# A hybrid retention and HGRN2 step: other pools for the last retention chunk, moved side work and loads, state updates in the output banks

## The chip, the cores and the metric

The kernel runs on one core of one Trainium2 chip. The metric is the device time of one execution in microseconds (us): the median of several runs. The engines are TensorE (PE in the profile; PEld is its weight load), VectorE (DVE), ScalarE (ACT), GpSimd (POOL) and SyncE (SP), which here issues most of the DMA transfers. PE works from on-chip memory (SBUF) into PSUM, which the kernel divides into four pools of two banks each.

## The reference

One layer mixes 2048 prompt tokens and 8 single decode tokens, with 1024 features. Eight projections of 512 columns feed two groups of four heads: retention with a fixed decay for each head, and HGRN2 with a learned decay for each token and feature. Their outputs are normalised, gated, joined and projected again.

```python
h = rmsnorm(x, norm_g)
p = (h @ w_in).astype(jnp.float32)          # 1024 x 4096
rq, rk, rv, rg, hq, hf, hi, hgate = jnp.split(p, 8, axis=-1)
rq, rk = rotary(rq, pos), rotary(rk, pos) * RET_DK ** -0.5
o_ret, s_ret_new = chunked_decay_recurrence(rq, rk, rv, log_gamma, s_ret)
o_ret = head_rmsnorm(o_ret, ret_g) * jax.nn.silu(rg)
logf = jnp.logaddexp(jnp.log(lbf), jnp.log1p(-lbf) + jax.nn.log_sigmoid(hf))
kin = (1.0 - lbf) * jax.nn.sigmoid(-hf)
o_hg, s_hg_new = chunked_decay_recurrence(silu(hq), kin, hi, logf, s_hg)
o_hg = head_rmsnorm(o_hg, hg_g) * jax.nn.silu(hgate)
y = x + jnp.concatenate([o_ret, o_hg], axis=-1) @ w_out      # then rmsnorm
# chunked_decay_recurrence: S_t = diag(f_t) S_{t-1} + k_t v_t^T ;  o_t = S_t^T q_t
```

Both the outputs and the new states of prompt and samples are returned.

## The kernel before

Every large product is made of float32 operands that are cut in two: `hi_lo` (L114) lets ACT copy the operand to a high part and DVE subtract that from the operand to get the low part, and `split` (L118) does so for a weight tile. A product is then three matmuls, high by high, high by low and low by high (`three`, L330).

The program has three stages. **Stage 1** is a loop over 24 token pairs, eight for each of three weight sets. A pair (`v_pair`) makes seven products of 12 matmuls of 512 columns each (the list `CHAIN`, named a to g in the tiles `pv18a` and so on), a scheme of the Strassen kind. The code of L864 to L930 hangs all other work of stage 1 on a list `after[n]`: what stands there is issued after product n of the pair (a half counts as in the middle). So the next weight set is loaded and summed (`wg_load`, `wg_spool`), the decode tokens get their matmuls by the raw weights (`wg_decode`, tile `pgd`, L576), the operands of the next pair are split (`s_split`), and the rotation table of the next pair is loaded into the single buffer `rot` (L361).

With the third set, 16 chunks of 128 tokens of the retention are woven in, two for each pair (`r_steps`, L775): `r_load` brings the chunk's `rq`, `rv` and `rg` into one buffer each (L704), `r_flip` transposes the keys (`pkt`), `r_score` multiplies keys and queries (`par`, L717) and masks the result on DVE (`rA`, L719), `r_update` makes the new part of the state (`pur`), `r_out` makes the output (`por`, L730 and L732) and updates the state `rS` on DVE (L736), `r_norm` normalises the output (`obr`, L752), which needs the square sums of ACT and two steps of POOL (`omr`, L744), and `r_turn` transposes it (`potr`, L760). The last chunk, 15, lies behind the last pair, among the first matmuls of stage 2.

**Stage 2** has eight units, two halves of the prompt by four heads. A unit multiplies its two weight tiles by the split activations (`pjfh` and `pjqh`, L966). Between these matmuls `merge` puts the recurrence of the unit before: the products of the levels inside of a chunk (`plh`, L1174 and L1224), fed by DVE and ACT (`kh` L1144, `qqh` L1147, `kept` L1154), and the tail (`tail_steps`): `uu` makes the state updates (`puh`, L1049) in a bank of the pool `ps_lv` that it shares with the levels, DVE chains them into states (`sth`, L1057), and `oo` makes the outputs in `ps_o`. The activations lie in four blocks; those of block 1 (`x_split`, low part `xl`) are made at the start of unit 0, before its second half needs them.

The list `side_at` (L1348) places side work at fractions of a unit: 4.8 is at 80% of unit 4. It holds the decode states of the four HGRN2 heads (`d_load`, two `d_mul`, `d_add`, `d_mm`) and the sums of the output weights for stage 3 (`t_load_raw`, four `t_sum`, `t_spool`, `t_store`). **Stage 3** projects the outputs: four plain chunks (`out_steps`, `py`, L1548), each from the outputs read back from memory (tile `or`) and split (`oc_h`, `oc_l`), and then six token pairs by seven products again.

PE follows the order of the program as written. DVE, ACT, SP and POOL are put in order by a scheduler from the waits and its model; `behind(f)` (L124) ties the instructions of f behind the last ones that DVE, ACT and SP had so far. Each engine then runs its list strictly in order, and SP's list is that of its DMA queue's issues. All loads of raw weights, states and activations share the pool `rawp` of six buffers.

Of the kernel before, what the change touches and what calls it, by code (L numbers as in the profile page):

```python
# [18 lines left out]
P = 128  # L19
# [22 lines left out]
def step_kernel(ctx, tc, a, out):  # L42
# [99 lines left out]

    def w_load():
        if len(w_ready) < len(want):
# [7 lines left out]
            r = rawp.tile([P, D], F32, tag="raw", name=f"wr{n}")  # L152
            sp.dma_start(r, a["w_in"][j])
            w_ready.append(split(r, f"w{n}_"))
# [210 lines left out]
    def v_pair(i, after):  # L365
# [8 lines left out]
        def emit(c, ty, ps, plus):  # L374
            key = n_set == 2 and ty == 0
            if key:
                pl, tag = (abp, "zh0") if c % 2 else (vq, "rk")
# [317 lines left out]
    def r_begin():  # L695
        for x, tag in (("kT", "zl0"), ("rA", "zh1"), ("rS", "zl1")):
            zz[x] = abp.tile([P, GW], F32, tag=tag, name=x)
# [29 lines left out]
    def r_out(c):  # L727
# [11 lines left out]
        o = vq.tile([P, GW], F32, tag="vo", name=f"obr{c}", bufs=3)  # L739
# [27 lines left out]
    def r_last():  # L767
        sf = vq.tile([P, GW], F32, tag="vo", name="sf", bufs=3)
# [6 lines left out]
    def r_steps(p):  # L775
# [20 lines left out]
        if p == N_V - 1:  # L796
            put(6, lambda: r_flip(ca + 1))
        if p:
            put(0.5 if p > 1 else 1.5, lambda: r_turn(ca - 2))
        if p < N_V:  # L800
# [46 lines left out]
    def d_mm(hd):  # L847
        S, vb = dec["l", hd]
        ty, h = divmod(hd, NH)
        sp.dma_start(out[("new_ret_sample", "new_hgrn_sample")[ty]][0, :, h].rearrange("b d v -> d b v"), S)  # L850
# [8 lines left out]
        for i in range(2):  # L859
            sp.dma_start(d_dram[hd, i::2], e[i : i + 103 : 34, i * P : i * P + P])  # L860
# [3 lines left out]
    for i in range(2, n_tok):  # L864
# [164 lines left out]
    def tail_steps(half, hd, acol, qcol, vcol, kT, decay, box, eps, gcol, name, ksb, ns):  # L1029
# [320 lines left out]
    for hd, at in zip(range(NH, 2 * NH), (4.8, 5.4, 6.0, 6.6)):  # L1350
# [489 lines left out]
```

## Time and profile before

| | us |
|---|---|
| runs | 1065.56, 1071.47, 1071.89 |
| median | 1071.47 |
| profiled execution | 1070.63 |
| its span in the trace | 1068.8 |
| PE busy | 1036.6 |
| DVE busy | 764.0 |
| ACT busy | 549.6 |
| POOL busy | 128.5 |

The profile shows one execution. Its span runs from the first to the last instruction; the 1.8 us to the execution's own time lie around it. Busy times are sums of intervals, and an instruction counts as busy while it runs, at whatever clock. In the views, L717 is line 717 of the kernel before, `A <- B` in a list of waits says that an instruction on A waited for one on B, and a name such as `pv18a` stands for the tile that is written. Stage 1 lies at 0 to about 590 us, stage 2 at about 580 to 915, stage 3 behind it.

### The profile page before, as it was taken

The numbers are of one execution on the slowest core, as the hardware profiler recorded it, in microseconds if no ns is written. First come the engines' busy times: TensorE is split into PE (matmuls) and PEld (weight loads), VectorE is DVE, ScalarE is ACT, GpSimd is POOL, SyncE is SP. The second block draws the span as 40 slices with busy tenths as digits, with TensorE's granted clock in tenths as the row PEclk, the third lists the DMA queues.
The fourth block names the chain that finished last, engine by engine and source line by source line (L and its number), as shares of the span: only waits on it lengthen the run. The fifth ranks groups of instructions, "written<-read, shape, count | busy, mean of one in ns | idle before, by whom it ended". The sixth has DMA issues, their size and how long they took to land.

```text
span 1068.8 us, 21293 instructions
## 1 busy us (share of the span) xinstructions
PE 1036.6 (97%) x8231; PEld 853.6 (80%) x8231; DVE 764.0 (71%) x1404; ACT 549.6 (51%) x1203; POOL 128.5 (12%) x224
## 2 busy tenths in 40 slices
PE   9999999999999999999999999999999999999997
PEld 7778678887778788788888888897777777888775
DVE  6886775987667976667657677867666687468785
ACT  7853445543344755544555565565455384433241
POOL 0310101000001011111111100011011012221122
PEclk9999999999999999999999999999999999999999
DMA  8689999568768775767677399673736465496642
GB/s 290 212 299 331 327 336 321 216 245 287 272 217 289 289 234 168 227 210 200 226 242 234 147 308 319 224 232 130 227 120 200 165 205 165 133 352 201 234 159 99
DMA packets 147270, 248.27 MB, mean 232 GB/s; under 512 B 10752, under 2 KB 78608, under 8 KB 146912
## 3 DMA queue, kind: packets, MB, share of 16 engines
q1 hardware_dynamic: 139696, 221.37, 61.9%
q0 software_dynamic: 7328, 25.27, 6.2%
q8 instruction: 65, 1.06, 0.4%
q14 instruction: 37, 0.30, 0.1%
q10 hardware_dynamic: 144, 0.26, 0.1%
HBM read 162.32 MB, written 84.54 MB: 231 GB/s over the span
## 4 chain that ended last, share of the span: by engine, by line
PE 66%; DMA 11%; DVE 9%; ACT 7%; issue 4%; POOL 1%; SPq 1%; DVEq 0%; POOLq 0%; ACTq 0%
PE po L332 11%; PE pjfh L966 5%; PE pjqh L966 4%; PE py L1548 3%; DMA rq<-qt_dram 2%; DMA xn<-in_x_prompt 2%; DMA qt_dram<-qt 2%; DMA wgr<-in_w 2%; PE par L717 1%; PE por L730 1%; PE plh L1174 1%; PE por L732 1%; PE pur L724 1%; PE puh L1049 1%; PE pv22a L332 1%
## 5 line engine op out<-in xcount | busy, mean ns | idle before, releaser
L966 PE MATMUL pjfh<-xh,w_h 128*128 128x512 f32 (+2 forms) x160 | 61.1, 382 | 0.1
L966 PE MATMUL pjqh<-xh,w_h 128*128 128x512 f32 (+2 forms) x160 | 59.8, 374 | 0.0
L1154 ACT ACTIVATE kepth<-kh 128x1024 f32<-128x1024 f32 x24 | 25.4, 1059 | 66.9 <-DVE kh L1144 62.6
L966 PE MATMUL pjfh<-xl,w_h 128*128 128x512 f32 (+2 forms) x160 | 56.9, 355 | 1.7 <-DVE xl L116 1.7
L966 PE MATMUL pjqh<-xh,w_l 128*128 128x512 f32 (+2 forms) x160 | 56.5, 353 | 1.5 <-DVE w_l L116 1.5
L966 PE MATMUL pjfh<-xh,w_l 128*128 128x512 f32 (+2 forms) x160 | 56.6, 354 | 0.0
L966 PE MATMUL pjqh<-xl,w_h 128*128 128x512 f32 (+2 forms) x160 | 56.2, 352 | 0.0
L1144 DVE TENSOR_TENSOR kh<-kh,fph 128x512 f32<-128x512 f32 x48 | 33.4, 695 | 23.8 <-PE plh L1174 14.8
L752 DVE SCALAR_TENSOR_TENSOR obr<-por,omr,rg 128x128 f32<-128x128 f32 x64 | 18.1, 345 | 34.9 <-POOL omr L744 32.5
L116 DVE TENSOR_TENSOR ab_l<-xr,ab_h 128x512 fp32r<-128x512 f32 (+1 forms) x40 | 37.5, 953 | 5.4 <-ACT ab_h L115 5.3
L115 ACT ACTIVATE ab_h<-xr 128x512 fp32r<-128x512 f32 (+1 forms) x40 | 32.3, 839 | 12.7 <-DVE xr L286 12.6
L1076 DVE SCALAR_TENSOR_TENSOR obh<-poh,orsh,v 128x128 f32<-128x128 f32 x64 | 18.0, 345 | 26.2 <-POOL orsh L112 23.7
L966 PEld LDWEIGHTS pjfh<-xh,w_h 128*128 128x128 f32 x160 | 30.7, 192 | 6.8 <-issue 2.5
L966 PEld LDWEIGHTS pjqh<-xh,w_l 128*128 128x128 f32 x160 | 30.3, 189 | 6.2 <-DVE w_l L116 1.9
L966 PEld LDWEIGHTS pjfh<-xl,w_h 128*128 128x128 f32 x160 | 30.7, 192 | 5.0 <-DVE xl L116 2.3
L966 PEld LDWEIGHTS pjfh<-xh,w_l 128*128 128x128 f32 x160 | 30.7, 192 | 4.3
L966 PEld LDWEIGHTS pjqh<-xh,w_h 128*128 128x128 f32 x160 | 30.2, 189 | 4.0 <-issue 0.4
L286 DVE SCALAR_TENSOR_TENSOR xr<-xr,g_in,rb 128x256 f32<-128x256 f32 x64 | 26.7, 479 | 8.7 <-DMA xr<-in_x_t 6.2
L1147 DVE TENSOR_TENSOR qqh<-qqh,fph 128x512 f32<-128x512 f32 x48 | 32.8, 684 | 0.0
L966 PEld LDWEIGHTS pjqh<-xl,w_h 128*128 128x128 f32 x160 | 30.3, 190 | 2.9
L762 ACT ACTIVATE obr<-potr,pk 128x128 f32<-128x128 f32 x64 | 18.5, 367 | 23.6 <-PE potr L760 23.6
L1638 DVE SCALAR_TENSOR_TENSOR xro<-xro,yms,fg 128x1024 f32<-128x1024 f32 (+1 forms) x13 | 15.6, 1203 | 20.5 <-POOL yms L112 20.5
(1835 smaller groups left out, 3406.5 us busy)
## 6 DMA issues: line engine op xcount, KB each, us to landing
xr<-a_dram SPq DMA_DIRECT2D x24, 512.0 KB
S<-s_dram SPq DMA_DIRECT2D x24, 512.0 KB
xn<-in_x_prompt SPq DMA_DIRECT2D x32, 256.0 KB
xr<-in_x_t SPq DMA_DIRECT2D x16, 512.0 KB
a_dram<-xr SPq DMA_DIRECT2D x16, 512.0 KB
s_dram<-S SPq DMA_DIRECT2D x16, 512.0 KB
wgr<-in_w SPq DMA_DIRECT2D x16, 512.0 KB
xr<-a_dram SPq DMA_DIRECT2D x32, 256.0 KB
```

Source lines behind the costliest of these rows:

```text
L115: act.activation(h, src, AF.Copy)
L116: dve.tensor_tensor(l, src, h.bitcast(F32), op=ALU.subtract)
L286: dve.scalar_tensor_tensor(r[:, k], r[:, k], g_in[:, kk : kk + 1], spread_to[i], op0=ALU.mult, op1=ALU.mult)
L332: pe.matmul(ps, xx, ww, start=(first and n == 0), stop=(last and n == 2), skip_group_check=more)
L752: dve.scalar_tensor_tensor(o[:, cc], po[:, h], ms[:, h : h + 1], rb_of[c, "g"][:, cc], op0=ALU.mult, op1=ALU.mult)
L762: act.activation(o[:, cc], pt[:, h], AF.Copy, scale=ng[:, h : h + 1])
L966: pe.matmul(ps, ww[:, kk], x[:, k, b0 : b0 + n], start=(k == 0 and i == 0), stop=(k == KT - 1 and i == 2),)
L1076: dve.scalar_tensor_tensor(ob[g][:, j], po[:, j], rs[:, j : j + 1], gcol(4 * g + j), op0=ALU.mult, op1=ALU.mult)
L1144: dve.tensor_tensor(kv[:, :, 0, :], kv[:, :, 0, :], two[:, :, 1:2].to_broadcast([P, nb, b]), op=ALU.mult)
L1147: dve.tensor_tensor(qv[:, :, 1, :], qv[:, :, 1, :], two[:, :, 0:1].to_broadcast([P, nb, b]), op=ALU.mult)
L1154: act.activation(ss[:, 512:], k[:, :HALF], AF.Copy)
L1548: pe.matmul(ps, o[:, kk], w[:, k % 4, i * 512 : (i + 1) * 512], start=(k == 0 and n == 0), stop=(k == KT - 1 and n == 2),)
```

## The change

What it does, by parts:

1. **Pools.** The tiles `kT`, `rA`, `rS` and the odd chunks' keys (tags z) move from the pool `abp` to `vq`, and the last chunk's `obr` and `sf` to `rawp`. So `abp` can be closed, and the memory of activation block 1 opened, before the last retention chunk. The splits of block 1 (`x_steps(1)`) are now issued one by one among the first steps of unit 0, and one split of block 0 moves there. `obr` of the last chunk is normalised earlier and transposed later.
2. **Weights.** The load of a weight tile (`w_fetch`) is separate from its split.
3. **Retention.** For pairs 1 to 6 of the third set the first chunk's `r_score` and `r_update` stand after product 5 instead of 4.5; for pairs 1 to 7 `r_out` and the loads of the second chunk's `rq` and `rv` stand after product 6 instead of 5.5.
4. **Decode.** `wg_decode` and `wg_spool` stand after product 4 instead of 3. The small stores of `d_mm` go to POOL's queue for the HGRN2 heads.
5. **State updates.** `puh` is taken from `ps_o` instead of `ps_lv`.
6. **Side work.** `side_at` gets other times, and the steps of one head or one quarter stand further apart.
7. **Output stage.** The loads of w_out's rows and of the first two chunks `or` stand in unit 7, ahead of the splits that use them; in stage 3 the loads and splits of later chunks are separate as well.

```diff
-    vt = vctx.enter_context(tc.tile_pool(name="vt", bufs=1))
     actx = ExitStack()
+    vt = actx.enter_context(tc.tile_pool(name="vt", bufs=1))
...
-    a21 = [[abp.tile([P, 4, P], F32R, tag=f"z{t}{n}", name=f"a21{t}{n}") for t in "hl"] for n in range(2)]
+    a21 = [[vq.tile([P, 4, P], F32R, tag=f"z{t}{n}", name=f"a21{t}{n}") for t in "hl"] for n in range(2)]
...
-        o = vq.tile([P, GW], F32, tag="vo", name=f"obr{c}", bufs=3)
+        if c < 2 * N_V - 1:
+            o = vq.tile([P, GW], F32, tag="vo", name=f"obr{c}", bufs=3)
+        else:
+            o = rawp.tile([P, GW], F32, tag="raw", name=f"obr{c}")
...
-            put(4.5 + d, lambda: r_score(ca), lambda: r_update(ca))
+            put(5 if 0 < p < N_V - 1 else 4.5 + d, lambda: r_score(ca), lambda: r_update(ca))
             if p:
-                put(5.5, lambda: r_out(ca), lambda: r_load(ca + 1, "q"), lambda: r_load(ca + 1, "v"))
+                put(6, lambda: r_out(ca), lambda: r_load(ca + 1, "q"), lambda: r_load(ca + 1, "v"))
+        if p == N_V - 1:
+            put(6, lambda: r_flip(ca + 1))
...
+        q = pool if ty else sp
...
-            sp.dma_start(d_dram[hd, i::2], e[i : i + 103 : 34, i * P : i * P + P])
+            q.dma_start(d_dram[hd, i::2], e[i : i + 103 : 34, i * P : i * P + P])
...
-                after[3] += [lambda m=m, k=j - 3: wg_decode(m, k), lambda m=m, k=j - 3: wg_spool(m, k)]
+                after[4] += [lambda m=m, k=j - 3: wg_decode(m, k), lambda m=m, k=j - 3: wg_spool(m, k)]
...
-            for kp in range(4):
-                after[2 + kp] += [lambda kp=kp: behind(lambda: x_split(0, kp, x_raw[0, kp]))]
-            after[4] += [w_load]
+            for kp, at in enumerate((1.5, 2.5, 3.5, 7)):
+                if at > 6:
+                    continue
+                after.setdefault(at, [])
+                after[at] += [lambda kp=kp: behind(lambda: x_split(0, kp, x_raw[0, kp]))]
+            after[4] += [w_fetch]
...
-            pu = ps_lv.tile([P, 4, P], F32, tag="lv", name=f"pu{name}{g}")
+            pu = ps_o.tile([P, 4, P], F32, tag="o", name=f"pu{name}{g}")
...
-    for hd, at in zip(range(NH, 2 * NH), (4.8, 5.4, 6.0, 6.6)):
+    for hd, at, mm in zip(range(NH, 2 * NH), (5.1, 5.45, 6.1, 6.45), (0.68, 0.43, 0.68, 0.43)):
-        for f, d in zip(steps, (0, 0.06, 0.085, 0.11, 0.32)):
+        for f, d in zip(steps, (0, 0.1, 0.17, 0.24, mm)):
-    for k, at in enumerate((0.4, 1.0, 1.8, 2.5)):
+    for k, at in enumerate((0.35, 1.35, 2.35, 4.35)):
-        for f, d in zip(steps, (0, 0.1, 0.115, 0.13, 0.145, 0.17, 0.25, 0.25, 0.33)):
+        for f, d in zip(steps, (0, 0.12, 0.18, 0.24, 0.3, 0.4, 0.48, 0.5, 0.58)):
...
+    side_at += [*((7.35 + 0.02 * n, f) for n, f in enumerate(wo0[1])),
+                (7.3, lambda: o_load(0)), (7.48, lambda: o_split(0)), (7.8, lambda: o_load(1)),
+                (7.7, wo1[1][0]), (7.85, wo1[1][1])]
...
-        (7, 1): lambda: wo_steps(0),
+        (7, 1): lambda: [wo0[0]] + [lambda j=j: behind(wo0[2][j]) for j in range(4)],
...
-            for n, f in enumerate(early[:8]):
-                f()
-                if n in (0, 1, 2, 4):
-                    tail_f.pop(0)()
-            r_last()
             actx.close()
...
             x_alloc(1)
-            for f in x_steps(1) + early[8:]:
+            side1 = [lambda: x_split(0, 3, x_raw[0, 3]), w_load] + x_steps(1)
+            behind(side1.pop(0))
+            for n, f in enumerate(early):
                 f()
-            r_norm(2 * N_V - 1)
-            tail_f.pop(0)()
+                if n in (0, 1, 2, 5):
+                    tail_f.pop(0)()
+                if n == 5:
+                    r_last()
+                    r_norm(2 * N_V - 1)
+                for f in side1[: 2 if n < 3 else 1]:
+                    behind(side1.pop(0))
             scan_pools()
+            fill.insert(8, (0, tail_f.pop(0)))
...
-    o_load(0)
-    o_load(1)
-    wo1 = wo_steps(1)
+    o_split(1)
     wo1[0]()
```

How the instructions move shows at three places. On SP at the end of the last token pair, around the loads for the last retention chunk (`rq`, `rv`, `rg`), the order before is this; `w_kept` are stores of split weights, `wr` a raw weight tile, `wot` raw output weights, and `kg_dram<-vo` the last pair's two output stores:

```order
L166 DMA w_keptl<-w_l 128x1024
L153 DMA wr_5598<-in_w_in 128x1024
L704 DMA rq_5428<-qt_dram 128x512
L704 DMA rv_5430<-v_dram_95 128x512
L1270 DMA wot_5675<-in_w_out 128x1024
L704 DMA rg_5483<-qg_dram_100 128x512
L1482 DMA fg<-in_final_norm_g 128x1024
L166 DMA w_kepth<-w_h 128x1024
L326 DMA kg_dram_104<-vo_5438 128x512
L326 DMA kg_dram_104<-vo_5443 128x512
```

The same place in the change, where `xr` are raw activations (its line numbers are shifted by the added lines, here by 7):

```order
L711 DMA rv_5312<-v_dram_95 128x512
L711 DMA rq_5310<-qt_dram 128x512
L711 DMA rg_5348<-qg_dram_100 128x512
L186 DMA xr_5465<-a_dram_109 128x2x256
L186 DMA xr_5465<-a_dram_110 128x2x256
L711 DMA rv_5440<-v_dram_95 128x512
L333 DMA kg_dram_104<-vo_5403 128x512
L333 DMA kg_dram_104<-vo_5408 128x512
L711 DMA rq_5438<-qt_dram 128x512
L711 DMA rg_5486<-qg_dram_100 128x512
L173 DMA w_kepth<-w_h 128x1024
```

The load of the last chunk's `rq` (5428 before, 5438 now) stood ahead of the two stores and now stands behind them; `wot` and the final norm's `fg` are gone from here.

On DVE at the start of unit 0, where block 1 is split (`xl<-xr`, `w_l` is the second weight tile's low part), the last chunk's work stands before as follows:

```order
L719 SCALAR_TENSOR_TENSOR rA<-par_5507,pk 128x128 x4
L736 SCALAR_TENSOR_TENSOR rS<-rS,pur_5516 128x128 x4
L770 TENSOR_SCALAR sf<-rS 128x128 x4
L752 SCALAR_TENSOR_TENSOR obr_5549<-por_5536,omr_5550,rg_5483 128x128
L116 TENSOR_TENSOR xl_5586<-xr_5462,xh_5585 128x2x512
L116 TENSOR_TENSOR xl_5586<-xr_5465,xh_5585 128x2x512
L116 TENSOR_TENSOR xl_5586<-xr_5468,xh_5585 128x2x512
L116 TENSOR_TENSOR xl_5586<-xr_5471,xh_5585 128x2x512
L116 TENSOR_TENSOR xl_5586<-pk,xh_5585 128x8x8
L752 SCALAR_TENSOR_TENSOR obr_5549<-por_5536,omr_5550,rg_5483 128x128 x3
```

And in the change:

```order
L957 MEMSET Ah 128x1024
L116 TENSOR_TENSOR xl_5186<-xr_5196,xh_5185 128x2x512
L116 TENSOR_TENSOR w_l<-wr_5350,w_h 128x1024
L116 TENSOR_TENSOR xl_5474<-xr_5456,xh_5473 128x2x512
L726 SCALAR_TENSOR_TENSOR rA<-par_5520,pk 128x128
L116 TENSOR_TENSOR xl_5474<-xr_5459,xh_5473 128x2x512
L116 TENSOR_TENSOR xl_5474<-xr_5462,xh_5473 128x2x512
L726 SCALAR_TENSOR_TENSOR rA<-par_5520,pk 128x128 x3
L116 TENSOR_TENSOR xl_5474<-xr_5465,xh_5473 128x2x512
L116 TENSOR_TENSOR xl_5474<-pk,xh_5473 128x8x8
L743 SCALAR_TENSOR_TENSOR rS<-rS,pur_5529 128x128 x4
L780 TENSOR_SCALAR sf<-rS 128x128 x4
```

Block 1's splits (`xl_5586` before, `xl_5474` now) stood behind all of the last chunk's state work; now they begin ahead of its `rA`, one by one between the masks, and `obr` of the last chunk comes last.

On DVE between units 6 and 7, ahead of the last unit's levels, the order before has the split of the first output chunk (`oc_l`) in the middle of the level work:

```order
L1137 COPY dech_8959<-fph_8951 128x8
L1019 TENSOR_TENSOR qqh_8571<-pjqh_512_8859,qsh_8947 128x512
L1021 TENSOR_TENSOR qqh_8571<-qqh_8571,fh_8569 128x512
L116 TENSOR_TENSOR oc_l<-or_9446,oc_h 128x1024
L1144 TENSOR_TENSOR kh_8570<-kh_8570,fh_8569 128x512
L1147 TENSOR_TENSOR qqh_8571<-qqh_8571,fh_8569 128x512
L1194 TENSOR_TENSOR Abh_8976<-pah_8977,pk 128x256
```

In the change:

```order
L1151 COPY dech_8959<-fph_8951 128x8
L1033 TENSOR_TENSOR qqh_8569<-pjqh_512_8849,qsh_8947 128x512
L1035 TENSOR_TENSOR qqh_8569<-qqh_8569,fh_8567 128x512
L1158 TENSOR_TENSOR kh_8568<-kh_8568,fh_8567 128x512
L1161 TENSOR_TENSOR qqh_8569<-qqh_8569,fh_8567 128x512
L1208 TENSOR_TENSOR Abh_8976<-pah_8977,pk 128x256
L1194 COPY_PREDICATED Abh_8976<-lmask,pah_8977 128x128
```

The split has left this place, so that `kh` follows `qqh` directly.

More of the change, by code (lines that the diff above doesn't have):

```diff
@@ L141, in step_kernel, with w_fetch @@
     w_used = [0]
+    w_raw = {}
+    def w_fetch():
+        n = len(w_ready)
+        w_raw[n] = rawp.tile([P, D], F32, tag="raw", name=f"wr{n}")
+        sp.dma_start(w_raw[n], a["w_in"][want[n]])
     def w_load():
@@ L151, in w_load @@
                 return
-            r = rawp.tile([P, D], F32, tag="raw", name=f"wr{n}")
-            sp.dma_start(r, a["w_in"][j])
-            w_ready.append(split(r, f"w{n}_"))
+            if n not in w_raw:
+                w_fetch()
+            w_ready.append(split(w_raw.pop(n), f"w{n}_"))
             for t, x in zip(w_ready[-1], w_kept):
@@ L696, in r_begin @@
         for x, tag in (("kT", "zl0"), ("rA", "zh1"), ("rS", "zl1")):
-            zz[x] = abp.tile([P, GW], F32, tag=tag, name=x)
+            zz[x] = vq.tile([P, GW], F32, tag=tag, name=x)
     heads = [slice(h * P, (h + 1) * P) for h in range(NH)]
@@ L767, in r_last @@
     def r_last():
-        sf = vq.tile([P, GW], F32, tag="vo", name="sf", bufs=3)
+        sf = rawp.tile([P, GW], F32, tag="raw", name="sf")
         for h, cc in enumerate(heads):
@@ L795, in r_steps @@
             put(5, lambda: r_turn(cb))
-        if p == N_V - 1:
-            put(6, lambda: r_flip(ca + 1))
         if p:
@@ L1403, in unit @@
                 if (i, n) in sides:
-                    group = weave(group, sides[i, n](), 0.0, 1.0 if i != 3 or n == 1 else 0.6)
+                    group = weave(group, sides[i, n](), 0.0, 1.0 if i not in (3, 7) or (i, n) == (3, 1) else 0.6)
                 steps += group
@@ L1521, in junk @@
         return pools["tp"].tile([P, 512], F32, tag="tmp", name=f"yj{junks[0]}")
-    oc = {}
-    def o_load(c):
-        r = rawp.tile([P, 8, P], F32, tag="raw", name=f"or{c}")
-        sp.dma_start(r, o_dram[:, :, c * P : (c + 1) * P].rearrange("h p t -> p h t"))
-        oc[c] = split(r.rearrange("p h t -> p (h t)"), f"oc{c}_")
     def out_steps(c):
@@ L1551, in part @@
                     )
+            if (kh, i, s) == pairs[1] + (1,) and c + 2 < PLAIN:
+                o_load(c + 2)
+            if (kh, i, s) == pairs[3] + (0,) and c + 2 < PLAIN:
+                behind(lambda: o_split(c + 2))
             if (kh, i, s) == pairs[1] + (0,):
@@ L1705, in step_kernel @@
     fill = place(fill, sorted([
-        *((0.02 + 0.04 * n, s) for n, s in enumerate(wo1[1:])),
+        *((0.02 + 0.04 * n, lambda s=s: behind(s)) for n, s in enumerate(wo1[2])),
+        (0.03, wo1[1][2]), (0.07, wo1[1][3]),
         (0.2, d_norm), (0.6, t2_load), (0.65, lambda: op_load(p0)), (0.75, lambda: op_s12(p0)),
```

29 lines of the change are left out of this document (17 added, 12 removed).

## The prediction

> **What bounds the kernel now.** I read the page first, then the list of PE's waits, then windows and timelines around the longest of them. The page's span, busy times and the foot of its chain:
>
> ```profile
> span 1068.8 us, 21293 instructions
> PE 1036.6 (97%) x8231; PEld 853.6 (80%) x8231; DVE 764.0 (71%) x1404; ACT 549.6 (51%) x1203; POOL 128.5 (12%) x224
> PE 66%; DMA 11%; DVE 9%; ACT 7%; issue 4%; POOL 1%; SPq 1%; DVEq 0%; POOLq 0%; ACTq 0%
> ```
>
> PE is busy for 97% of the span. The change leaves PE's 8231 instructions as they are in number and shape, so it can move only what PE does not work: 1068.8 − 1036.6 = 32.2 us at the most, and the time lost at a low clock, which hides inside the busy time. PE's waits, grouped by what released them (total, times, longest):
>
> ```profile
> PE puh L1049 <- DVE sth L1057: 3.8, 4, 1.4
> PE pgd L576 <- DMA wgr<-in_w: 2.7, 5, 0.6
> PE par L717 <- DMA rq<-qt_dram: 2.4, 4, 1.2
> PE plh L1174 <- ACT kepth L1155: 2.3, 1, 2.3
> PE pjfh L966 <- DVE xl L116: 1.7, 2, 1.6
> PE pjqh L966 <- DVE w_l L116: 1.5, 1, 1.5
> PE puh L1049 <- issue: 1.1, 1, 1.1
> PE pkh L1041 <- DVE kh L1144: 1.0, 1, 1.0
> PE plh L1224 <- DVE qqh L1147: 0.9, 1, 0.9
> PE py L1548 <- DVE wol L1442: 0.9, 1, 0.9
> PE por L730 <- DVE rA L719: 0.6, 1, 0.6
> PE par L717 <- DVE xl L116: 0.6, 1, 0.6
> PE plh L1174 <- DVE Abh L1180: 0.6, 1, 0.6
> ```
>
> No wait is long; the loss is some twenty small ones, each where an edit of this change lies. Two of them cost more than they show. The windows (length, busy time of PE, PEld, DVE, ACT and POOL, then the granted clock, the DMA share and GB/s) behind the waits of 1.6 and 2.3 us:
>
> ```profile
> 590.00:600.00 10.00, 8.26 (x47) 6.69 (x46) 5.48 (x13) 6.57 (x16) 1.98 (x3) 0.97 0.44 162
> 600.00:610.00 10.00, 10.00 (x74) 9.98 (x74) 6.83 (x13) 3.98 (x11) 0.81 (x1) 0.86 0.07 28
> 845.00:849.00 4.00, 4.00 (x16) 3.43 (x16) 1.36 (x6) 1.32 (x3) 0.00 (x0) 0.57 0.03 9
> ```
>
> The clock lost is 10 × 0.03 + 10 × 0.14 = 1.7 us in the first place, and 4 × 0.43 = 1.7 us in the second.
>
> A wait also costs its restart. PE's timeline around the last pair (start, duration, tile):
>
> ```profile
> 569.83 0.39 PE L332 MATMUL pv23e<-B22l,s231h 128*128 128x512 f32 x1
> 570.06 0.39 PE L332 MATMUL pv23e<-B22h,s231l 128*128 128x512 f32 x1
> 571.04 1.13 PE L717 MATMUL par<-rq,kT 128*128 128x128 f32 x8 [0.59 <-DVE xl L116]
> 578.70 0.48 PE L332 MATMUL pv23c<-T1h,s231h 128*128 128x512 f32 x1
> 580.17 0.60 PE L709 MATMUL pkt<-ident,rk 128*128 128x128 f32 x4
> 580.53 0.48 PE L966 MATMUL pjfh<-xh,w_h 128*128 128x512 f32 x1
> ```
>
> Undisturbed matmuls start 570.06 − 569.83 = 0.23 us apart; across the wait it is 0.98. The loss is 0.75 where the wait is put at 0.59, so each wait costs 0.16 us more.
>
> **The change part by part: what goes.** *State updates in ps_o.* The second `puh` of a unit waits for a bank that DVE's chain of states still reads:
>
> ```profile
> 653.19 1.23 DVE L116 TENSOR_TENSOR w_l<-wr,w_h 128x1024 fp32r<-128x1024 f32 x1
> 654.82 0.32 DVE L1057 SCALAR_TENSOR_TENSOR sth<-sth,dech,puh 128x128 f32<-128x128 f32 x1
> 655.20 1.16 PE L1049 MATMUL puh<-v,ksh 128*128 128x128 f32 x8 [1.38 <-DVE sth L1057]
> ```
>
> The chain ends at 655.14, drawn out by a split of 1.23 us in its middle, and `puh` starts right behind. In `ps_lv` the banks go pa, pu, pl, pu, so the second pu takes the first one's bank back; in `ps_o` the two updates take both banks one after the other, and what held them is the unit before's output. All five waits go, 3.8 + 1.1 = 4.9 us; and the levels, which no longer share, lose the 0.6 of `Abh`. What is late next is `poh`, which takes the first update's bank and also needs the states that come out of it, so its own operands hold it as long as the bank does.
>
> *Decode matmuls* one product later: 12 matmuls × 0.23 = 2.8 us more for a load that was at most 0.6 late. Of 2.7 us I keep 0.3.
>
> *Retention.* `par` comes 6 matmuls later (half a product, 1.4 us), against a longest wait of 1.2: the 2.4 us for `rq` go. At the last pair x's splits come half a product sooner, which takes the 0.6 of `par` on `xl` and the 0.6 of `por` on `rA`.
>
> *Block 1 split sooner.* Before, DVE makes the four low parts in one stretch, behind the last chunk:
>
> ```profile
> 596.48 4.62 DVE L116 TENSOR_TENSOR xl<-xr,xh 128x1024 fp32r<-128x1024 f32 x4
> ```
>
> Now the first of them stand ahead of that chunk's `rA`, so the waits of 1.7 on `xl` go, with the first fall of the clock. The 1.5 on `w_l` goes as its load is taken off its split.
>
> *Output loads and splits apart.* In unit 7 the split of `or` sits in ACT's and DVE's lists ahead of the levels, and its load is late:
>
> ```profile
> 831.50 7.90 DMA or<-o_dram
> 840.51 1.22 DVE L116 TENSOR_TENSOR oc_l<-or,oc_h 128x1024 fp32r<-128x1024 f32 x1 [4.18 <-ACT oc_h L115]
> 842.43 1.06 ACT L1154 ACTIVATE kepth<-kh 128x1024 f32<-128x1024 f32 x1 [1.96 <-DVE kh L1144]
> 844.10 0.74 PE L1174 MATMUL plh<-kepth 128*32 128x16 f32 x64 [2.26 <-ACT kepth L1155]
> ```
>
> DVE stood for 4.18 us, then `kh`, `kepth` and `plh` came late. In the new order the split is no longer there: the 2.3 go, with the second fall of the clock. The new split stands about half a unit behind its load, some 20 us against 7.9.
>
> *Side work spread.* Of `pkh` 1.0, `qqh` 0.9 and `py` 0.9, each behind queued side work or a late split, I take half, 1.4.
>
> The sum: 4.9 + 2.4 + 2.4 + 1.7 + 0.6 + 0.6 + 1.5 + 2.3 + 0.6 + 1.4 = 18.4 us of waits. They are about 22.5 in number, × 0.16 = 3.6 for restarts, and 3.4 for the clock: 25.4 us.
>
> **What comes.** *`potr` of chunk 14.* Its `por` moves half a product nearer to its turn. The rows above show `por` giving way at 578.70, and DVE:
>
> ```profile
> 581.59 1.13 DVE L752 SCALAR_TENSOR_TENSOR obr<-por,omr,rg 128x128 f32<-128x128 f32 x4 [2.23 <-POOL omr L744]
> ```
>
> `obr` ends at 582.72, 4.0 us after `por`. Between the two PE now has 12 matmuls, 2.8, and `pkt`, 580.53 − 580.17 = 0.4: 0.9 us of new wait; nothing below zero, since `por` cannot finish later for it.
>
> *`rq` of chunk 15* stands behind two output stores in SP's list, which wait for the last product:
>
> ```profile
> 586.59 0.92 SPq L326 DMA_DIRECT2D kg_dram<-vo  x2
> 447.73 5.63 DMA rq<-qt_dram
> ```
>
> Issued at 587.5 and landing 5.6 later, at 593.1, it can hold PE for 0 to 2 us, as `por` of this chunk stands about there now; I take 0.7.
>
> *The units.* Side work has the same instructions at other times, and its new neighbours can be hit as the old were. Bounds are 0 and 8.9, the sum of the six unit waits above whose releaser stood behind side work or late splits, with `py` (1.7 + 1.5 + 2.3 + 1.0 + 0.9 + 0.9 = 8.3) and `Abh` (0.6). I take three waits like `pkh`, 3.0 us, the small ones of the list.
>
> With 0.4 for their restarts new waits are 5.0 us. *At nothing* I put: the stores of `d_mm` on POOL, which is busy for 12%; `rq` in the other pairs, which comes behind the rotation table in SP's list (its cover is the stretch between that and `par`, priced as a rival below); and block 1's memory opened sooner, whose tiles' last readers are the last pair's matmuls, ahead on PE anyway.
>
> 25.4 − 5.0 = 20.4. The profiled execution becomes 1070.6 − 20.4 = 1050.2. It lies 0.8 under the median of the runs, so the forecast is 1051.
>
> **The rivals.** *The clock falls stay.* The waits go and the falls turn up elsewhere, after other small ones: 3.4 us more, 1054.4. For it: PE keeps small waits, and nothing shows how small is safe. Against: the falls came behind waits of 1.6 and 2.3 us, and the stretch with the wait of 1.5 on `w_l` kept its clock at 1.00:
>
> ```profile
> 626.00:636.00 10.00, 8.51 (x163) 6.50 (x162) 8.64 (x15) 5.98 (x11) 0.00 (x0) 1.00 0.81 286
> ```
>
> The Trainium skill ("TensorE: Matmul & The Clock Gate", What's actually happening) says that the clock halves after an idle window of about 3.4 us in a window that runs free. By that rule neither fall would have come from a wait of 1.6 or 2.3 us alone, and removing these need not remove the falls; the trace disagrees with it on the size of the gap, and agrees on the length of the slow stretch: 4 × 0.43 / 0.5 = 3.4 us.
>
> *Side work only changes place.* DVE keeps its 764 us and ACT its 550, so the unit waits come back at other tiles. Of the gains in units (4.9 + 1.7 + 1.5 + 2.3 + 0.6 + 1.4 = 12.4, with about 2 of restarts and 3.4 of the clock) 70%, less the 3.0 already counted, come back: some 10 us, 1062 with rounding. Against: the puh waits have a bank as their cause, not a place.
>
> *All goes and nothing comes*: 1070.6 − 25.4 + 0.8 = 1046, and 1045 with the other half of `pkh` and its like.
>
> *Slower: `rq` behind the rotation table.* Seven pairs now issue the second chunk's `rq` behind `rot` on SP, and `rot`, with its one buffer, waits for DVE's rotation of the pair before:
>
> ```profile
> 430.08 0.87 SPq L704 DMA_DIRECT2D rq<-qt_dram  x1
> 435.82 0.33 SPq L361 DMA_DIRECT2D rot<-in_rot  x1
> 441.23 1.05 PE L717 MATMUL par<-rq,kT 128*128 128x128 f32 x8
> ```
>
> If `rot` comes no sooner than now, `rq` is issued at 436.15. With 5.63 us it lands at 441.8, 0.6 after `par`; with the 7.9 of the `or` load at 444.0, 2.8 after. Beyond 2.3 us a wait brings a fall of the clock too: 2.8 + 1.7 + 0.2 = 4.7 in each pair, × 7 = 33 us, 1084. It decides from about 2.3 us of lateness on, and makes the kernel slower than before where it passes 20.4 / 7 = 2.9 us a pair. Against: `por` now comes later, so DVE turns the product before `obr`, and `rot` comes one to two us sooner; `rq` then lands about 1 us ahead of `par`.
>
> **How the numbers follow.** The forecast gets 0.57, all gone 0.08, the clock rival 0.10, side work 0.19, the slower rival 0.06. One per cent, about what a measurement can tell from no change, is 10.7 us: faster lies below 1060.8. The first three are faster, 0.75; side work is within one per cent, 0.19; the last is slower, 0.06. The range goes from 1044, a us below the case in which all goes, to 1066, four us above the side-work case for what the unit bound leaves (8.9 where 3.0 is taken); it leaves out the slower rival and some of the tails.
>
> **What would show it.** In the changed kernel: no `puh` wait on `sth`; `pgd` and `par` waits under 0.5 us in all; a clock of 0.99 in both windows; PE idle within the span down by about 17 us; a wait of about 1 at `potr` near the end of the last pair. Waits of `par` on `rq` of over 2 us in each pair would show the slower rival, and new waits at `plh`, `pkh` or `pjfh` of over 9 us together the side-work one.

## The result and the profile after

| | before | changed |
|---|---|---|
| median of 20 runs, us | 1070.84 | 1064.48 |
| lowest and highest, us | 1065.56, 1075.86 | 1060.70, 1067.43 |
| span of the profiled execution, us | 1068.8 | 1062.7 |

The ratio is 0.994, with a 95% interval of 0.9926 to 0.9954: 6.4 us faster, where 20 were forecast. The head of the page of the changed kernel:

```profile
span 1062.7 us, 21303 instructions
PE 1037.7 (98%) x8231; PEld 855.2 (80%) x8231; DVE 762.9 (72%) x1404; ACT 548.5 (52%) x1203; POOL 132.9 (13%) x232
```

PE is busy 1.1 us longer than before with the same instructions; the windows below show three stretches at a low clock where the kernel before had two (beside one at the very end in both). PE's idle time fell from 32.2 to 25.0 us, by 7.2 where about 17 were forecast. The waits of PE in the changed kernel (total, times, longest):

```profile
PE pv8a L339 <- ACT s L379: 2.1, 1, 2.1
PE pkt L716 <- DVE rk L364: 2.1, 1, 2.1
PE pv4a L339 <- ACT u L379: 1.9, 1, 1.9
PE plh L1188 <- ACT kepth L1169: 1.5, 1, 1.5
PE plh L1188 <- DVE Abh L1194: 1.5, 1, 1.5
PE pah L1206 <- DVE qqh L1035: 1.3, 1, 1.3
PE pv2b L339 <- DVE ab_l L116: 1.2, 1, 1.2
...
PE py L1572 <- DVE wol L1460: 1.0, 3, 0.4
PE pv8b L339 <- ACT wv_h L115: 0.9, 1, 0.9
PE pv8b L339 <- DVE wv_l L116: 0.8, 1, 0.8
PE plh L1238 <- DVE qqh L1161: 0.4, 1, 0.4
```

What the list of before led with is gone: no `puh`, no `pgd`, no `par` on `rq`, no `pjfh` on `xl`, no `pjqh` on `w_l`. In their place stand waits in stage 1 that the list of before does not have: `pv4a`, `pv8a`, `pv8b`, and a longer `pkt` (2.1 against 0.4). Windows of the changed kernel over the three new places and over the two old falls of the clock (the columns are those of the prediction's windows):

```profile
105.00:125.00 20.00, 18.11 (x84) 13.76 (x83) 14.48 (x25) 8.59 (x17) 2.15 (x3) 0.91 0.86 324
185.00:205.00 20.00, 16.27 (x64) 11.94 (x63) 17.13 (x21) 14.10 (x17) 0.39 (x1) 0.91 0.83 324
365.00:385.00 20.00, 17.76 (x83) 14.35 (x82) 15.96 (x22) 10.67 (x18) 0.00 (x0) 0.91 0.61 203
590.00:610.00 20.00, 19.79 (x137) 17.94 (x136) 14.12 (x28) 12.51 (x32) 2.80 (x4) 1.00 0.63 224
840.00:850.00 10.00, 10.00 (x128) 8.65 (x121) 4.92 (x12) 5.07 (x14) 0.58 (x1) 1.00 0.02 8
```

Both old falls are gone (1.00 in the last two rows), and there are three new ones, each 20 × 0.09 = 1.8 us. Where the time went shows best in the starts of the stages, read off PE's timeline: the start of the first matmul of a pair (`pv4a` for pair 4), of unit 0 (`pjfh`) and of stage 3 (`py`), and the end of the last matmul, in us. The letter in `pv4a` is that of the product's bank in PSUM, and not, as was said ahead, that of the product: products are counted from 0, and products 0, 2, 4 and 6 of pair 4 all go by `pv4a`. The last two columns belong to experiments below.

| | before | changed | e1_sums_back | e12_rotd_early |
|---|---|---|---|---|
| pair 4 | 98.16 | 98.96 | 98.66 | 99.54 |
| pair 5 | 120.41 | 123.50 | 120.23 | 124.14 |
| pair 8 | 182.83 | 184.48 | 183.61 | 184.76 |
| pair 9 | 202.93 | 210.97 | 203.70 | 204.88 |
| pair 16 | 349.85 | 356.94 | 350.32 | 351.75 |
| pair 17 | 373.21 | 383.63 | 374.84 | 375.82 |
| pair 23 | 550.29 | 557.12 | 548.12 | 550.04 |
| unit 0 | 580.53 | 585.73 | 576.73 | 579.17 |
| stage 3 | 874.89 | 867.93 | 861.43 | 861.67 |
| end | 1061.33 | 1055.18 | 1048.64 | 1048.88 |

The changed kernel loses 2.3 us in pair 4 (the differences are 0.8 ahead of it and 3.1 behind), 6.4 in pair 8 and 3.3 in pair 16. It wins 3.6 in pairs 17 to 22, 1.6 in pair 23 and 12.2 in the units, and loses 0.8 in stage 3. So most of the gains came, and 12 us that the prediction did not have went against them in stage 1.

### The profile page after: what moved, and what is told of

Its sections match the earlier page's. It is cut to its first block, busy times and chain, and to the rows that moved or that the text cites. A ratio compares the mean times of both kernels' runs of the same rounds, so it can differ in the third digit from the quotient of the medians.

```text
span 1062.7 us, 21303 instructions
## 1 busy us (share of the span) xinstructions
PE 1037.7 (98%) x8231; PEld 855.2 (80%) x8231; DVE 762.9 (72%) x1404; ACT 548.5 (52%) x1203; POOL 132.9 (13%) x232
## 5 line engine op out<-in xcount | busy, mean ns | idle before, releaser
L752 ACT ACTIVATE obr<-por 128x128 f32<-128x128 f32 x64 | 16.8, 277 | 44.0 <-PE por L739 30.8
```

## The experiments

Two theories stood against each other: the decode matmuls and weight sums that moved one product later make the losses of stage 1, or the new pools and late transfers do.

**The sums back, and the sums alone.** One edit, undone in the changed kernel, and made alone in the kernel before:

```diff
-                after[4] += [lambda m=m, k=j - 3: wg_decode(m, k), lambda m=m, k=j - 3: wg_spool(m, k)]
+                after[3] += [lambda m=m, k=j - 3: wg_decode(m, k), lambda m=m, k=j - 3: wg_spool(m, k)]
```

> The changed kernel with the decode matmuls and the weight sums (wg_decode, wg_spool) back after product 3. Theory A: putting them one product later made the new waits of pairs 4, 8 and 16 (pv4a 1.9, pv8b 0.9 and 0.8, pv8a 2.1, pkt 2.1 us, three falls of the clock of 1.7 each), 12 us by the starts of the pairs, and saved some 3.5 us at pgd. So those waits go, the pgd waits of about 2.7 us come back, and the time falls by about 8 us to 1056. Rival B: the new waits come from the tiles' new pools or from transfers that happen to be late, not from this edit: the waits stay and the time is within 2 us of 1064.5, or 3 us above it by the pgd waits.

Measured: 1055.19 us beside 1070.09 of the kernel before, ratio 0.9858 (0.9832 to 0.9884). This is what theory A said. The list of waits has no `pv4a`, `pv8a` or `pv8b`; the table shows pair 8 as long as before. The `pkt` wait of pair 16 stays at 1.5, without a fall of the clock, and of that pair's loss of 3.3 us 1.2 stay.

```profile
PE pgd L583 <- DMA wgr<-in_w: 3.0, 4, 1.1
...
PE pkt L716 <- DVE rk L364: 1.5, 1, 1.5
```

> The kernel before with this one edit, decode matmuls and weight sums after product 4. Theory A: about 12 us of new waits in pairs 4, 8 and 16 less 3.5 at pgd, some 8 us slower than before, 1079. Rival B: only the pgd waits go, 2.4 us and their restarts, 1068.

Measured: 1077.53 us beside 1070.09, ratio 1.0064 (1.004 to 1.0089), 7.4 us slower, with the same waits in pairs 4 and 8:

```profile
PE pv8a L332 <- ACT s L372: 2.1, 1, 2.1
...
PE pv4a L332 <- ACT u L372: 1.6, 1, 1.6
```

From both sides this edit makes the loss of pair 8 (6.8 us here, by the starts of the pairs) and the wait of pair 4; the pools do not. In pair 4 the wait cost only 0.5 us here, as no fall of the clock followed it. Pair 16 is another matter: the edit alone lost 0.8 there, so it does not account for all of the 3.3.

**Decode back, sums late.** Only `wg_decode` goes back after product 3.

> The changed kernel with the decode matmuls alone back after product 3, the sums and their stores still after product 4. Theory A1: the wait of pair 4 (pv4a on ACT's u) was hidden before by the decode matmuls that stood there, and those of pairs 8 and 16 come from the sums' stores, which hold up the loads of the next weight set. So pv4a's 1.9 us and its fall of the clock go, pgd's 2.7 us come back, pairs 8 and 16 keep their waits: within 1.5 us of 1064.5. Rival A2: the late matmuls themselves (the raw tiles held longer) are what delays pairs 8 and 16: those waits go too, about 1056.

Measured: 1057.91 us, ratio 0.9885 (0.986 to 0.9911). The waits of pair 4 and, against A1, those of pair 8 are gone; the time lies nearer to A2's 1056. The sums overwrite the raw tiles that the decode matmuls read, so the place of the matmuls decides when the sums run: in DVE's timeline the last sum of pair 6 starts 1.5 us ahead of pair 7 here, 1.9 ahead in the kernel before, and 2.1 behind its start in the changed kernel. What is left above e1_sums_back is a loss of 3.0 us in pair 6, at `pgd`, with a fall of the clock.

**Half a product.**

```diff
-                after[4] += [lambda m=m, k=j - 3: wg_decode(m, k), ...]
+                after.setdefault(3.5, []).extend([lambda m=m, k=j - 3: wg_decode(m, k), ...])
```

> The changed kernel with the decode matmuls and the sums in the middle between, after half of product 4 (1.4 us later than before, 1.4 us sooner than in the change). Theory A: each us that the sums come later is a us that the next set's loads come later, against a slack that the kernel before still had, and the loads bind only beyond it: the pgd waits (at most 1.1) go, the waits of pairs 4 and 8 stay away or stay under 1 us without a fall of the clock: 1053 to 1056. Rival B: the loss grows in proportion to the delay: half of 9.3 us, about 1060.

Measured: 1059.37 us, ratio 0.9905 (0.9877 to 0.9933). The time is B's, but the loss is not in proportion to the delay: by the starts of the pairs, pair 8 loses 2.1 us where it lost 6.4, pair 4 loses 0.6 and keeps its wait of 1.8 (without a fall of the clock), and pair 16 loses 3.7, no less than before, after a `pkt` wait of 2.4 with a fall. So B's number came by luck. The wait of pair 4 has its own cause, which the traces show. ACT and PE of the kernel before in pair 4:

```profile
110.22 0.58 ACT L372 ACTIVATE u<-pv4a 128x512 f32<-128x512 f32 x1
110.34 0.62 PE L576 MATMUL pgd<-wgr,pk 128*8 128x256 f32 x8 [0.64 <-DMA wgr<-in_w]
111.57 0.62 PE L576 MATMUL pgd<-wgr,pk 128*8 128x256 f32 x8 [0.62 <-DMA wgr<-in_w]
112.12 0.50 PE L332 MATMUL pv4a<-T3h,s40h 128*128 128x512 f32 x1
```

And of the changed kernel:

```profile
110.01 0.63 ACT L263 ACTIVATE xn<-xn 128x512 f32<-128x512 f32 x1 [4.57 <-DMA xn<-in_x_prompt]
111.77 0.57 ACT L379 ACTIVATE u<-pv4a 128x512 f32<-128x512 f32 x1
112.40 0.74 PE L339 MATMUL pv4a<-T3h,s40h 128*128 128x512 f32 x1 [1.90 <-ACT u L379]
```

ACT reads the bank of `pv4a` out late, since a squaring of `xn` stands ahead of it and waits for a load, in both kernels (for 3.8 us before). Before, PE was in the decode matmuls meanwhile: moved away, their `pgd` waits of 1.3 us here would only have given way to a wait for `u` of about as much. With the matmuls behind product 4, PE stands in front of the bank.

**What makes pair 8 late.** The page of before shows nothing of it, so its parts were taken out one by one. First the read-out of the decode matmuls, whose store stands on SP ahead of the later ones of the next set's loads (`wg1B`). In the changed kernel ACT ends it late: its second half waits for a store of `vo`, and two stores of `vo` stand on SP behind the four stores of the late sums:

```profile
171.87 0.77 ACT L527 ACTIVATE gd<-pgd 8x256 f32<-8x256 f32 x2 [2.85 <-DMA v_dram<-vo]
```

The edit in the changed kernel:

```diff
-                after[0] += [lambda m=m: wg_decode_out(m)]
+                after[2] += [lambda m=m: wg_decode_out(m)]
```

> The changed kernel (late sums) with wg_decode_out, the read-out of the decode matmuls, after product 2 of the set's last pair instead of product 0. Theory A: what makes pair 8 late is SP's list: the read-out's store to dg_dram waits for ACT, which waits for a store of vo, which stands behind the late sums' stores; and the second pair of wg1B loads stands behind dg_dram. With dg_dram behind those loads they are issued some 4 us sooner, and of pair 8's 6.4 us (pv8b 0.9 and 0.8, pv8a 2.1, the fall of the clock) at least 4 go: 1060. Rival B: the loads wait for a raw buffer that the late sums hold; then they are issued as late as before and the time stays at 1064.5.

Measured: 1063.47 us, ratio 0.9937 (0.9919 to 0.9955): no gain, as B had it, but not by B's mechanism. The second pair of loads left SP at 170.80 and not at 175.21 (2.9 us sooner, counted from the start of pair 7), but another wait took the place of the old ones, on DVE's split instead of ACT's:

```profile
PE pv8a L339 <- DVE wv_l L116: 3.5, 1, 3.5
```

DVE's timeline shows what that split stood behind, a load of 8 rows, `rotd`:

```profile
182.62 0.68 DVE L359 TENSOR_TENSOR t0d<-gd,rotd 8x512 f32<-8x512 f32 x1 [3.56 <-DMA rotd<-in_rotd]
...
185.64 3.48 DVE L116 TENSOR_TENSOR wv_l<-wg1B,wv_h 128x1024 fp32r<-128x1024 f32 x3
```

The same load in the kernel before:

```profile
171.57 0.68 DVE L352 TENSOR_TENSOR t0d<-gd,rotd 8x512 f32<-8x512 f32 x1 [1.35 <-DMA rotd<-in_rotd]
...
176.45 2.36 DVE L116 TENSOR_TENSOR wv_l<-wg1B,wv_h 128x1024 fp32r<-128x1024 f32 x2 [2.35 <-ACT wv_h L115]
```

Changed:

```profile
173.33 0.68 DVE L530 TENSOR_TENSOR gd<-gd,gds 8x512 f32<-8x512 f32 x1
180.75 0.68 DVE L359 TENSOR_TENSOR t0d<-gd,rotd 8x512 f32<-8x512 f32 x1 [6.74 <-DMA rotd<-in_rotd]
...
182.94 2.34 DVE L116 TENSOR_TENSOR wv_l<-wg1B,wv_h 128x1024 fp32r<-128x1024 f32 x2
```

In the changed kernel DVE stands for 6.7 us in front of `rotd`, and the splits that PE needs stand behind it in its list. The issues of SP and POOL suggest why that load is slow. Before, `rotd` leaves ahead of the 512 KB loads `T2l`:

```profile
170.05 0.29 SPq L528 DMA_DIRECT2D rotd<-in_rotd  x1
170.86 0.78 POOL L551 DMA_DIRECT2D T2l<-ws1T  x1 [31.88 <-DMA wg1B<-in_w]
```

Changed, it leaves behind them:

```profile
172.51 0.78 POOL L558 DMA_DIRECT2D T2l<-ws1T  x1 [28.69 <-PE pv7a L339]
173.85 0.55 POOL L558 DMA_DIRECT2D T2l<-ws1T  x1 [0.56 <-DMA wg1B<-in_w]
174.45 0.29 SPq L535 DMA_DIRECT2D rotd<-in_rotd  x1
```

Before, the first reader of `rotd` starts 171.57 − 170.05 = 1.5 us after the issue; changed, 180.75 − 174.45 = 6.3. The other runs that leave the load in its place agree: it took 1.4 to 1.6 us to the first reader in the seven profiles in which `rotd` left ahead of the second `T2l`, and 4.1 to 8.9 in the five in which both `T2l` had left before it. The exception is e8_half, where it left ahead of them, but 1.1 us behind two `wg1B` loads, and the reader came after 4.9. So it is large transfers sent shortly ahead that go with a late `rotd`; which of them delays it was not tried. The next two runs load `rotd` one pair sooner, where it needs nothing and nobody waits:

```diff
+            if j == 6:
+                after[0] += [lambda m=m: rotd_load(m)]
             if j == 7:
                 after[0] += [lambda m=m: wg_decode_out(m)]
```

> The changed kernel (late sums) with the small load rotd (8x128, the rotation of the decode tokens) one pair sooner, ahead of the traffic of the next set. Theory A: in pair 7 of the change DVE stood 6.7 us for rotd and had all splits of the next weights (wv_l) behind it; that is one half of pair 8's lateness, the late loads of wg1B the other. So DVE's wait goes, its first wv_l starts some 5 us sooner, and the waits of pair 8 shrink to what the wg1B loads still make, 1 to 4 of 6.4 us: 1059.5 to 1063. Rival B: the loads alone decide and DVE's wait hid behind them: 1064.5.

Measured: 1057.34 us beside 1068.69 of before, ratio 0.9899 (0.9869 to 0.9929): with the sums still late, 4.4 us faster than the change by the two ratios and 7.1 by the medians, a little below A's range. By the table pair 8 is as long as before (20.1 us); pair 4 keeps its loss. DVE of this run:

```profile
167.47 0.67 DVE L359 TENSOR_TENSOR t0d<-gd,rotd 8x512 f32<-8x512 f32 x1
...
178.37 2.36 DVE L116 TENSOR_TENSOR wv_l<-wg1B,wv_h 128x1024 fp32r<-128x1024 f32 x2 [5.81 <-ACT wv_h L115]
```

The lists of other engines moved too: the store to `dg_dram` now left SP at 171.49 and not at 174.04, and the later loads of `wg1B` at 172.99 and not at 175.21. So this run takes away both causes, the slow `rotd` and the late loads, and e10_out_later only a part of the second.

> The changed kernel (late sums) with both: rotd one pair sooner, and wg_decode_out after product 2, so that the second pair of wg1B loads isn't behind its store on SP. Theory A: with both causes gone pair 8 loses at most 1.5 of its 6.4 us: 1058 to 1059.5, 5 us faster than the change. Rival B: a third cause keeps pair 8 late (the sums' stores fill the DMA queues ahead of the wg1B loads): 1062 or more.

Measured: 1057.54 us, ratio 0.9895 (0.9867 to 0.9924), the same as without the second edit. By the starts of the pairs pair 8 loses 1.8 us here, with a `pv8a` wait of 1.5; no cause of 6 us is left. This run also parts the two causes, for it differs from e10_out_later by `rotd` alone: the second pair of `wg1B` loads leaves 6.8 us behind the start of pair 7 here and 6.9 there, the third pair 11.1 and 10.2. The loads came no sooner, and pair 8 lost 1.8 us instead of 6.6. So the slow `rotd`, with what the scheduler reorders around it, makes about 4.8 us of it. The rest goes with the late third pair: in e12_rotd_early all of these loads leave within 9.3 us, and nothing is lost.

**The state updates in the output banks.** Undone in the changed kernel, and made alone in the kernel before:

```diff
-            pu = ps_lv.tile([P, 4, P], F32, tag="lv", name=f"pu{name}{g}")
+            pu = ps_o.tile([P, 4, P], F32, tag="o", name=f"pu{name}{g}")
```

> The changed kernel with the state updates back in the pool of the levels. Theory A: the waits of puh on sth come back, 4.9 us with 0.8 for restarts and 0.6 at the levels, about 6 us slower than the change, 1070.5. Rival B: the new places of the side work take DVE's splits out of the chain of states, and the puh waits went by that: within 1.5 us of 1064.5.

Measured: 1066.11 us, ratio 0.9964 (0.9948 to 0.9979), 1.6 us above the change by the medians and 2.6 by the ratios, between the two theories; of the `puh` waits two come back:

```profile
PE puh L1063 <- DVE sth L1071: 2.1, 2, 1.1
```

> The kernel before with one edit: the state updates in the pool of the outputs. Theory A: the shared bank makes the puh waits, so all five go, 4.9 us with 0.8 for restarts and 0.6 at the levels: 6 us faster, 1064. Rival B: DVE's splits make them, and with another bank the same lateness turns up at poh or at the next levels: at most 2 us faster, 1068 or more. The changed kernel lost only 1.6 us when this edit was undone there, which either would give if each edit alone takes most of the waits away.

Measured: 1065.84 us, ratio 0.9963 (0.9947 to 0.9979), 3.7 us faster than before, between the theories and nearer to A. No `puh` wait is left, and from the start of unit 0 to stage 3 the profiled execution is 4.9 us shorter. So the bank makes these waits. With the old bank the changed kernel has 2.1 us of them where the kernel before had 4.9; something else in the change makes them fewer. That it is the side work's new places is likely but was not tried, and the two gains in time, 2.6 and 4.0 us by the ratios, differ by no more than their intervals allow.

**The side work's times.** The list `side_at` of before in the changed kernel.

> The changed kernel with the old times of the side work (decode states and sums of the output weights); the output loads keep their new places. Theory A: the banks and the earlier splits made the gain in the units, and the spread is worth half of pkh and qqh, 1 us: 1064.5 to 1066.5. Rival B: the spread did most of it, as DVE's queue is what delays the levels and the states: 4 us or more slower than the change, 1068.5 or more, with new waits at plh and pkh.

Measured: 1063.22 us, ratio 0.9934 (0.9904 to 0.9964), not slower but 1.3 us faster than the change by the medians, which is within the intervals: the spread brought nothing that shows, not even A's 1 us.

**The retention edit alone.**

> The kernel before with the retention edit alone (par half a product later, por and the loads of the next rq and rv too). Theory A: the par waits on rq go, 2.4 us with 0.6 for restarts, against 0.9 at potr: 2 to 3 us faster, 1067.5. Rival B: rq, now behind the rotation table on SP, comes late for the second chunk's par: new par waits of over 1 us in several pairs, the same time or slower than 1070.

Measured: 1069.06 us, ratio 0.9998 (0.9978 to 1.0019): B's "same time", but not for B's reason. The `par` waits on `rq` are gone and pairs 17 to 23 are 4.3 us shorter, but a new wait, followed by a long fall of the clock, eats most of the gain:

```profile
PE potr L760 <- DVE obr L752: 7.0, 2, 6.2
```

ACT of this run shows what stands behind it, at the squares for chunk 14's `obr`:

```profile
582.12 0.28 ACT L742 ACTIVATE obr<-por 128x128 f32<-128x128 f32 x1 [8.12 <-DMA o_dram<-obr]
```

They wait 8.1 us for the store of an earlier `obr`, whose buffer they take over. With `por` after product 6, two outputs of the pair are taken from the ring of three buffers ahead of `obr`, and the third place is that of chunk 13, whose store is on its way. In the changed kernel the order is the same and there is no such wait:

```profile
585.72 0.28 ACT L752 ACTIVATE obr<-por 128x128 f32<-128x128 f32 x1
```

There the store was issued at 582.55 and the squares start 3.2 us later; here it was issued at 573.44, and the DMA engines were 0.92 busy from 572 to 582. Which of the other edits makes the store quick was not tried. So the retention edit alone pays nothing, and in the changed kernel it pays what was forecast.

**Towards a better version.** First the early sums with the old side work; then, on the early sums, the `pkt` transposes half a product later; then the first with `rotd` early.

> The changed kernel with the decode matmuls and sums back after product 3, and the old times of the side work: both edits that brought nothing are taken out. Theory A: the two are independent, so the time is that of the sums alone (1055.2) less 1 us, about 1054. Rival B: with stage 1 at another phase the side work's old places hit the levels again: 1057 or more.

Measured: 1053.66 us beside 1069.80 of before, ratio 0.9847 (0.9823 to 0.9871), as A had it. The step from e1_sums_back is 1.2 us by the ratios, which the intervals do not tell from nothing.

> The kernel with the sums back after product 3 (1055.2), and the first chunk's key transposes and scores (pkt, par of chunk 0) half a product, 1.4 us, later. Theory A: the wait of pkt on rk of 1.5 us, which is there in all runs with 0.4 to 2.4 and comes from the rotation table's load, goes: 1.7 us faster, 1053.5. Rival B: par or pair 17 waits by as much instead, since keys and scores follow one another: 1055.

Measured: 1058.53 us, 3.3 above the kernel without it and above both theories. The `pkt` wait is gone, and the next matmul, which needs a split that stands behind the same work on DVE, waits 2.2 us with a fall of the clock (`pv16c` on `B22l`).

> The kernel with the sums back after product 3 and the old side work (1053.7), with rotd one pair sooner as well. Theory A: with early sums nothing waits long behind rotd (pair 8 had no waits), so nothing changes: 1053 to 1055. Rival B: rotd cost there too, in DVE's order: 1052 or less.

Measured: 1053.50 us beside 1068.69, ratio 0.9853 (0.9824 to 0.9882), the same as without `rotd` early. These two versions beat both kernels, the changed one by 9 to 11 us.

## Why the prediction was wrong

**The step that failed** is "*Decode matmuls* one product later", which stood in the sum as a gain: 2.4 us of waits and 0.8 of restarts. The `pgd` waits did go; none is left. But of the moved step only the matmuls were counted. Behind them lie the four sums on DVE, their four stores on SP, the read-out with its store, and the load `rotd`, and none was followed to who waits for it; the step had no cost and no rival. Undone, it was worth 9 us (1064.48 to 1055.19), and alone it cost 7.4. Stage 1 up to pair 17 came out 10.4 us longer, where 3.2 shorter was in the sum: 13.6 of the 14 us by which the forecast missed. Not all of that is the step's. 0.8 lies in pair 2, at a `pv2b` wait, where the step moves nothing; that wait is between 0.3 and 1.4 us in the runs built on either kernel. And the `pkt` wait in pair 16 stays at 0.8 to 1.5 with early sums. There DVE stands for the rotation table, for 2.5 us before, 3.4 in the changed kernel and 3.7 in e1_sums_back; what makes the table later was not settled.

**The cover.** The same step was also a cover, for ACT's read-out of `pv4a`. The prediction asked what hides the edits at nothing, and not what the moved work was hiding.

**The clock.** Both old falls went, as forecast, 3.4 us. Three new ones came, after the new waits of 1.9, 2.1 and 2.1 us. So what the rival "the clock falls stay" describes did happen, by way of the failed step. That each of these waits brought a fall is in part chance: e13_rotd_early_out_later has waits of 1.9 at `pv4a` and 2.1 at `pkt` without one (the last section shows why).

**The retention edit** was put at 3.0 with restarts; pairs 17 to 22 show 3.6. The `potr` wait, put at 0.9, and that for the last `rq`, put at 0.7, did not come. (The restarts of the five new waits were put at 0.4; at the prediction's own 0.16 each they are 0.8.) The last pair with its earlier splits won 1.6.

**The units** were put at a gain of 17.8 us (12.4 of waits, about 2 of restarts, 3.4 of the clock) less 3.4 of new waits, 14.4; measured 12.2. The mechanism of the bank was right: 6.3 forecast with restarts and the levels, 4.9 by the trace of the edit alone. The 0.6 of `Abh` did not go with the shared bank, as the prediction had it; it is 1.5 in the changed kernel. The wait of 2.3 on `kept` went with the earlier output loads, but one of 1.5 came back in an earlier unit. Half of `pkh`, `qqh` and `py`, 1.4 us, was credited to the spread of the side work, and e7_old_side shows no gain from it.

**The slower rival**, `rq` behind the rotation table, did not happen: no `par` waits on `rq` in the changed kernel. Nor did the side-work rival: 12.2 of the 14.4 us came in the units.

**The range.** The measured 1064.5 lies inside the range of 1044 to 1066, but by luck: its upper end was drawn for side work that hits the units again, and the loss came in stage 1, at a step that was counted as a gain.

## What to carry to other kernels

When a step moves, follow everything that it issues, down to the smallest transfer, and ask what its engines' strict lists hold behind each; here a load of 8 rows, sent shortly behind large ones, held all weight splits on DVE. Ask also what the moved work was covering where it stood, since a wait on PE can hide another engine's lateness. And take a wait apart by single edits: one run with the loads sooner and one with `rotd` sooner as well showed which of two late things PE had stood for.

## What the runs showed of the hardware

The length of a wait does not say whether the clock falls behind it. Over the sixteen profiled kernels, up to the last microseconds, all of nine waits over 2.2 us were followed by a slow stretch, six of nine between 1.85 and 2.2 us, and two of 21 between 1.5 and 1.8 us. The same wait of 1.57 us, `pjfh` on `xl`, brought a fall in the kernel before and none in e2_sums_late_only.

What decides it is a fixed grid. The slow stretches last 3.41 us or twice that, at half clock, and within a run they start at multiples of 3.413 us from each other: in the changed kernel at 112.49, 194.41 and 375.32, which lie 24 and 53 such steps apart. Where the grid lies against the start of the kernel differs from run to run (the starts leave a remainder of 3.3 us in the changed kernel and of 2.1 in the kernel before). Cut along it, each window has the clock 1.00 or 0.50 throughout, and PE's busy time in one window goes with the clock of the next. Two windows of the changed kernel, then two of the kernel before and two of e2_sums_late_only around the wait of 1.57 us (the columns are those of the windows above):

```profile
109.08:112.49 3.41, 1.51 (x8) 0.94 (x6) 2.41 (x7) 2.41 (x7) 0.00 (x0) 1.00 0.88 336
112.49:115.90 3.41, 3.41 (x8) 2.70 (x9) 3.38 (x5) 2.50 (x5) 0.00 (x0) 0.50 0.92 311
596.01:599.42 3.41, 1.67 (x11) 1.31 (x11) 3.21 (x4) 3.20 (x5) 0.17 (x1) 1.00 0.00 0
599.42:602.83 3.41, 3.41 (x17) 3.20 (x16) 3.38 (x8) 0.06 (x1) 0.00 (x0) 0.50 0.00 0
604.01:607.43 3.42, 1.94 (x12) 1.54 (x12) 3.42 (x4) 2.64 (x5) 0.00 (x0) 1.00 0.00 0
607.43:610.84 3.41, 3.21 (x25) 3.01 (x26) 3.38 (x8) 1.35 (x5) 0.00 (x0) 1.00 0.00 0
```

In the kernel before the whole wait fell into one window, which left PE busy for 1.67 of 3.41 us; in e2_sums_late_only the edge at 604.01 cut the wait in two, and 1.94 were left. Over all sixteen traces, of the windows at full clock the next one was slow behind all 18 with up to 1.67 us of busy time, behind two of five with 1.68 to 1.79, and behind none of the 4717 with more. So a window that is busy for less than about half costs the next one its clock, 1.7 us, and a wait of 1.5 to 3 us is a matter of where it falls on the grid.

The Trainium skill ("TensorE: Matmul & The Clock Gate", What's actually happening) has the gate watch a free-running window of about 3.4 us, and the traces agree with that. Its rule that the clock falls after an idle window does not fit: the windows ahead of the falls of the changed kernel were busy for 1.3 to 1.5 us.
